# Keeping column-group products together on TensorE, with modulations two k-tiles at a time

## Chip, core and metric

The kernel runs on one core of a Trainium2 chip. The metric is the time of one execution in device microseconds; the time of a kernel is the median of its runs, and beside it stands one profiled execution, whose trace is read here.

## What is computed

A diffusion trunk of four layers over 256 latent and 256 context tokens of width 1024. Layer by layer the token mixer is windowed attention, a bidirectional Mamba-2, a bidirectional mLSTM and latent attention (MLA); after each comes a mixture of 16 small experts, two per token. Around every sub-layer the tokens are scaled, shifted and gated by a modulation, a linear map of the conditioning vectors:

```python
for i in range(DEPTH):
    mod_x = jax.nn.silu(c) @ w_mod[i] + b_mod[i]        # c: (1, 1024), w_mod[i]: (1024, 6144)
    mod_c = jax.nn.silu(c_ctx) @ w_mod[i] + b_mod[i]
    sh1x, sc1x, g1x, sh2x, sc2x, g2x = jnp.split(mod_x[:, None, :], 6, axis=-1)
    ...
    hx = rmsnorm(xs, norm1_g[i]) * (1.0 + sc1x) + sh1x
    yc, yx = mixer_i(hc, hx)                           # attention, Mamba-2, mLSTM, MLA
    xs = xs + g1x * yx
    hx = rmsnorm(xs, norm2_g[i]) * (1.0 + sc2x) + sh2x
    xs = xs + g2x * hier_moe(hx, ...)                  # the context tokens likewise
return rmsnorm(xs, final_norm_g)
```

All data is f32. The modulation weights are 24 MB a layer, read once each for two rows of input.

## The kernel before

Tokens stand as four tiles of 128 (two of context, two of latent). Large products use a split into two f32r halves and three products (`mm3`, lines 207 to 209); transposes and the small products of the mixers are plain f32. A compile-time scheduler sets the order of every engine's queue: it goes by the order of the program, takes work that its own estimate of time says is ready, and so interleaves work of different helpers. On the chip each engine then works through its queue in that order. Two means in the program bear on the order: `issue_after` ties the instructions of a block behind a given one on its engine, and `high_priority` lets a block go ahead of other ready work.

**Column groups.** A product whose result has only 32 or 64 rows fills 32 or 64 of TensorE's 128 columns. Such products are written to several groups of columns, each with its own rows of one PSUM bank, and groups can run side by side. Five places matter here:

- Modulations (line 231, tile `wm`): `mod_round(i, r)` computes a third (2048 columns) of layer i's modulation in eight steps, one per k-tile of 128 rows. A step loads one 1 MB tile `w` through `wload` (line 182, on SP's queue) and issues four products in four groups of 32 columns, each for 512 columns of the weights. After the eighth, `fin` adds the bias and spreads the result. There are three rounds a layer, 96 k-tiles in all.
- Attention values (line 1128): per token tile and key head, 4 or 8 products in two groups of 64 columns, for 2 or 4 key tiles `PT`.
- Mamba heads (line 1398): per pair of heads, 8 products, four chunks in two groups.
- mLSTM states (line 1635): 4 products in two groups, twelve times.
- MLA values (line 1927): per pair of heads, 8 products in two groups.

**Where modulations stand.** Round 0 of layer 0 runs at the start. The others are a list of steps, `fq`: rounds 1 and 2 of the layer and round 0 of the next. The mixers call `fill(n)` at fixed places, which takes n entries off the list; `drain` takes the rest at a mixer's end. The tiles `w` are a ring of four 1 MB buffers that modulation loads share with the weights of the mixers (and later of the experts), all issued on SP in one queue; a load waits for its buffer's last reader, and what is queued behind it waits too. In Mamba, SP's queue also carries the decay rows (`A`, line 1350; `E`, line 1354).

Of the kernel before, what the change touches and what calls it, by code (L numbers as in the profile page):

```python
# [23 lines left out]
class Trunk:  # L24
    def __init__(self, ctx, tc, I, K, out, slots=128, opts=None):
        self.ctx, self.tc, self.nc, self.I, self.K, self.out = ctx, tc, tc.nc, I, K, out
        self.o = dict(ring=4, eb=4, ob=6, wl=(8, 8, 8, 10), early=(5, 5, 3, 5), ahead=4, yb=3, fv=1, y0=0, mv=1, go=((0, 0), (1, 0), (2, 0), (0, 1), (3, 0), (1, 1), (2, 1), (3, 1)), cadd=(0, 512, 512, 0), mh=(8, 8, 4, 4), ms=3, mo=3, fm=(2, 2, 1, 0, 0, 0, 0, 6), sdp=0, pmw=1, pud=1, ac=1, fs=(3, 2, 2, 2, 1, 1, 1, 1, 2, 2, 2, 2, 1, 1, 2, 2), Mb=1, Wb=1, wa=4, fl=0, fc="1" * 16, fp=(4, 1), pg=(3,), pe=(0, 1, 2, 3), ptb=4, pb=8, n1p=0, lag=2, tl=4, cc=(1,), manual=False, stop=None)
        self.o.update(opts or {})
        self.C = slots
        self.fq, self.pending = deque(), None  # L30

# [165 lines left out]
    def split(self, pool, w, shape, name="split", bufs=3):  # L197
# [5 lines left out]
        return hi, lo  # L203

    def mm3(self, ps, a, b, start, stop):
        mm = self.nc.tensor.matmul
        mm(ps, a[0], b[0], start=start, stop=False)  # L207
        mm(ps, a[0], b[1], start=False, stop=False)  # L208
        self.last_mm = mm(ps, a[1], b[0], start=False, stop=stop)  # L209


    def mod_round(self, i, r):

        nc, I = self.nc, self.I
        st = {}

        def step(j, load=None):
            if j == 0:
                st["ps"] = self.P.tile([128, 512], F32, name="wm", bufs=1)
            if j == 6:  # L220
                st["b"] = (self.const if r == 2 else self.lay).tile([128, 512], F32, name=f"mod{r}", bufs=1)
                (nc.vector if self.o["mv"] else nc.gpsimd).memset(st["b"], 0.0)
                for s in range(2):
                    b = I["b_mod"]
                    src = bass.AP(tensor=b.tensor, offset=b.offset + i * 6 * D + r * 2048,
                                  ap=[[512, 4], [1, 512]])
                    nc.scalar.dma_start(st["b"][s:128:32, :], src)
            src = I["w_mod"][i].rearrange("(p j) n -> p j n", j=8)[:, j, r * 2048:(r + 1) * 2048]
            w = load([src]) if load else self.wload(src, [128, 2048])
            for g in range(4):  # L230
                nc.tensor.matmul(st["ps"][32 * g:32 * g + 32, :], self.cs[:, j, :], w[:, 512 * g:512 * g + 512],  # L231
                                 start=(j == 0), stop=(j == 7))

# [35 lines left out]

        return [lambda load=None, j=j: step(j, load) for j in range(8)] + [fin]  # L270

# [9 lines left out]
    def fill(self, n=1):  # L281
        for _ in range(n):
            if self.fq:
                self.fq.popleft()()

    def drain(self):
        while self.fq:
            self.fq.popleft()()

# [772 lines left out]
    def attn_core(self, pool, pout, kz, vr, qT):  # L1062
        nc, I, o = self.nc, self.I, self.o
# [44 lines left out]
        def values(t, kv, pr, sm):  # L1108

            nk = 2 if t < 2 else 4  # L1110
            tok = slice(t * 128, (t + 1) * 128)
            PT = [pool.tile([128, 2, 4, 128], F32, name="PT", bufs=o["ptb"]) for _ in range(nk // 2)]
            for g in range(4):
                p = pr[g][:, :nk * 128]
# [10 lines left out]
            po = self.core()  # L1125
            for k in range(nk):
                for par in range(2):
                    nc.tensor.matmul(po[par * 64:(par + 1) * 64, :256], vr[:, k, kv * 64:(kv + 1) * 64],
                                     PT[k // 2][:, k % 2, par::2, :], start=(k == 0), stop=(k == nk - 1))
            pv = po[:, :256].rearrange("p (m q) -> p m q", m=2)  # L1130
# [164 lines left out]
    def ssm_main(self, pool, late, mid, keep, heads):  # L1295
# [46 lines left out]
        def head(ft, zt, xs, xr, CT, Br, CB, gs, first):  # L1342
# [52 lines left out]
            py = self.core()  # L1395
            for c in range(4):
                for h in range(2):
                    nc.tensor.matmul(py[64 * h:64 * h + 64, tok(c)], xr[:, 128 * c + 64 * h:128 * c + 64 * h + 64],
                                     M[0][:, h, c, :], start=True, stop=True)
            y = xs  # L1400
# [208 lines left out]
    def mlstm_states(self, pool, keep, kT, va, gt):  # L1609
# [3 lines left out]
        st = {}  # L1613
# [12 lines left out]
        for d, order in ((0, (0, 1, 2, 3)), (1, (1, 0, 3, 2))):  # L1626
            for n in range(3):
                c, nx = order[n], order[n + 1]
                s = keep.tile([128, 4, 130], F32, name=f"cst{d}{n}")
                for ab in range(2):  # L1630
                    ps = self.core()
                    for a in (2 * ab, 2 * ab + 1):
                        for h in range(2):
                            hd = 2 * a + h
                            nc.tensor.matmul(ps[64 * h:64 * h + 64, (a % 2) * 130:(a % 2) * 130 + 130],
                                             kw[c, d][:, hd * 64:hd * 64 + 64], va[c][:, hd, :], start=True, stop=True)
                    for a in (2 * ab, 2 * ab + 1):
# [256 lines left out]
    def mla_core(self, pool, kT, vr, qT, ohi, olo):  # L1894
        nc, I = self.nc, self.I
        sc = 96.0 ** -0.5
        for a in range(8):
            po = self.core()
            PT = []
            for h in range(2):  # L1900
# [22 lines left out]
                PT.append(pt)  # L1923
            for k in range(4):
                for h in range(2):
                    hd = 2 * a + h
                    nc.tensor.matmul(po[64 * h:64 * h + 64, :256], vr[k][:, hd * 64:hd * 64 + 64],  # L1927
                                     PT[h][:, k].rearrange("p t q -> p (t q)"), start=(k == 0), stop=(k == 3))
            hh, ll = ohi[a // 2][:, a % 2, :], olo[a // 2][:, a % 2, :]
# [33 lines left out]
    def layers(self, dense=False):  # L1963
# [3 lines left out]
        for i in range(first, 4):  # L1967
# [3 lines left out]
            with self.pool("layer") as self.lay:  # L1971
                if i == first:
                    for n, f in enumerate(self.mod_round(i, 0)):
                        f()
                        if n == 3 and not dense:
                            self.load_x()
# [107 lines left out]
```

## Time and profile before

| what | value |
|---|---|
| median of 3 runs | 2065.24 us (2065.15 to 2068.01) |
| profiled execution | 2062.44 us |
| its span, first to last instruction | 2060.3 us |
| TensorE busy | 1899.6 us (92%) |
| VectorE, ScalarE, GpSimd busy | 1394.9, 1036.1, 536.4 us |
| mean granted TensorE clock | 0.963 of full speed |
| DMA, mean over the span | 229 GB/s |

In time order: start-up to 38 us, attention to 300, its experts to 500, Mamba to 950, its experts to 1170, mLSTM to 1460, its experts to 1700, MLA to 1880, and the last experts. Times in the trace count from the span's start. In a timeline of TensorE, PE is the products and PEld the weight loads that feed them; an f32 product appears as two records, an f32r product as one. A record's end is modelled and overlaps the next one's start, so costs are best read from start to start.

### The profile page before, as it was taken

How to read it: one execution, taken by the hardware profiler on the slowest of the kernel's cores; microseconds unless marked ns; L12 is line 12 of the kernel's file. 1: busy time of each engine (PE TensorE's matmuls, PEld its weight loads, DVE VectorE, ACT ScalarE, POOL GpSimd, SP SyncE). 2: the span in 40 equal slices, each digit the busy share in tenths (PEclk: the TensorE clock that was granted, in tenths of full speed). 3: DMA queues.
4: the chain of work that ended last, by engine and by line, in shares of the span. 5: the costliest groups of instructions: out<-in, count | busy, mean ns of one | idle time of the engine just before them, and what ended most of it. 6: DMA issues, size and time to landing. Idle time of an engine off the chain costs nothing. (4 is left out here: it accounts for less than half of the span.)

```text
span 2060.3 us, 30756 instructions
## 1 busy us (share of the span) xinstructions
PE 1899.6 (92%) x11036; PEld 1411.8 (69%) x11036; DVE 1394.9 (68%) x2728; ACT 1036.1 (50%) x2172; POOL 536.4 (26%) x525
## 2 busy tenths in 40 slices
PE   5999988999999999998799899996979999998996
PEld 2875686777767778776577678885867766656542
DVE  3568557886598787777788662338578876486444
ACT  2447526775575555433577542245457755454111
POOL 2012232213475555445221410004241132001000
PEclk8999998999999999999899999998989999999998
DMA  9344667986486546547798557542669966807792
GB/s 342 137 164 166 244 208 275 400 304 191 135 252 210 158 169 200 180 141 269 266 391 339 164 163 265 189 164 90 236 215 378 401 194 228 296 11 277 285 368 94
DMA packets 172915, 471.73 MB, mean 229 GB/s; under 512 B 27769, under 2 KB 74993, under 8 KB 152272
## 3 DMA queue, kind: packets, MB, share of 16 engines
q1 hardware_dynamic: 148912, 401.98, 54.3%
q0 software_dynamic: 23136, 65.86, 10.0%
q8 instruction: 90, 1.47, 0.3%
q10 hardware_dynamic: 704, 1.82, 0.2%
q14 instruction: 73, 0.60, 0.1%
HBM read 452.41 MB, written 29.77 MB: 234 GB/s over the span
## 5 line engine op out<-in xcount | busy, mean ns | idle before, releaser
L758 DVE TENSOR_TENSOR elo<-wl,ehi 128x1024 fp32r<-128x1024 f32 x156 | 187.0, 1220 | 27.8 <-ACT ehi L757 26.9
L757 ACT ACTIVATE ehi<-wl 128x1024 fp32r<-128x1024 f32 x156 | 161.6, 1055 | 51.8 <-PE acc L209 32.7
L231 PE MATMUL wm<-w,cs 128*32 128x512 f32 x768 | 125.2, 640 | 22.7 <-DMA w<-in_w_mod_dram 22.7
L763 POOL DMA_INDIRECT xg<-hd,gi x48 | 64.0, 1334 | 281.9 <-PE tr L776 224.0
L1292 POOL TENSOR_TENSOR wcl<-w,wch 128x512 fp32r<-128x512 f32 x76 | 114.2, 1515 | 81.8 <-ACT wch L1291 75.7
L207 PE MATMUL acc<-hhi,wch 128*128 128x512 f32 (+1 forms) x336 | 131.8, 393 | 0.5 <-ACT wch L1291 0.5
L209 PE MATMUL acc<-split_hi,hlo 128*128 128x256 f32 x464 | 131.3, 285 | 0.0
L209 PE MATMUL acc<-hhi,wcl 128*128 128x512 f32 (+1 forms) x336 | 129.8, 388 | 1.4 <-POOL wcl L1292 1.4
L208 PE MATMUL acc<-split_lo,hhi 128*128 128x256 f32 x464 | 131.0, 285 | 0.0
L207 PE MATMUL acc<-split_hi,hhi 128*128 128x256 f32 x464 | 131.0, 286 | 0.0
L208 PE MATMUL acc<-hlo,wch 128*128 128x512 f32 (+1 forms) x336 | 129.9, 387 | 0.0
L207 PE MATMUL acc<-ehi,xTh 128*128 128x512 f32 x288 | 123.6, 429 | 2.2 <-ACT xTh L779 2.2
L208 PE MATMUL acc<-elo,xTh 128*128 128x512 f32 x288 | 117.8, 409 | 1.1 <-DVE elo L758 1.1
L209 PE MATMUL acc<-ehi,xTl 128*128 128x512 f32 x288 | 115.6, 401 | 0.0
L758 DVE TENSOR_TENSOR elo<-w,ehi 128x1024 fp32r<-128x1024 f32 x84 | 100.9, 1218 | 13.6 <-ACT ehi L757 13.1
L757 ACT ACTIVATE ehi<-w 128x1024 fp32r<-128x1024 f32 x84 | 87.0, 1052 | 26.2 <-PE acc L209 14.8
L1370 ACT ACTIVATE A<-A,lnb 128x128 f32<-128x128 f32 x256 | 78.6, 388 | 39.4 <-POOL A L1365 39.4
L207 PEld LDWEIGHTS acc<-split_hi,hhi 128*128 128x128 f32 x464 | 88.1, 191 | 9.4 <-issue 3.5
L202 DVE TENSOR_TENSOR split_lo<-w,split_hi 128x1024 fp32r<-128x1024 f32 x33 | 40.1, 1224 | 80.3 <-ACT split_hi L201 80.0
L209 PEld LDWEIGHTS acc<-split_hi,hlo 128*128 128x128 f32 x464 | 88.5, 191 | 3.2 <-DVE split_lo L202 0.8
L386 POOL TENSOR_TENSOR x<-x,restmp 128x256 f32<-128x256 f32 (+1 forms) x46 | 48.2, 1047 | 160.1 <-DVE restmp L382 146.0
L208 PEld LDWEIGHTS acc<-split_lo,hhi 128*128 128x128 f32 x464 | 88.5, 191 | 0.7 <-issue 0.7
(625 smaller groups left out, 5456.9 us busy)
## 6 DMA issues: line engine op xcount, KB each, us to landing
w<-in_w_mod_dram SPq DMA_DIRECT2D x96, 1024.0 KB
wl<-in_moe_w_down_dram SPq DMA_DIRECT2D x47, 1024.0 KB
wl<-in_moe_w_gate_dram SPq DMA_DIRECT2D x82, 512.0 KB
wl<-in_moe_w_up_dram SPq DMA_DIRECT2D x82, 512.0 KB
w<-in_moe_w_gate_dram SPq DMA_DIRECT2D x46, 512.0 KB
w<-in_moe_w_up_dram SPq DMA_DIRECT2D x46, 512.0 KB
w<-in_ssm_w_in_dram SPq DMA_DIRECT2D x40, 512.0 KB
yd<-y POOLq DMA_DIRECT2D x39, 512.0 KB, 9.6
```

The costliest lines, as they stand in the source:

```text
L202: self.nc.vector.tensor_sub(lo, w, hi)
L207: mm(ps, a[0], b[0], start=start, stop=False)
L208: mm(ps, a[0], b[1], start=False, stop=False)
L209: self.last_mm = mm(ps, a[1], b[0], start=False, stop=stop)
L231: nc.tensor.matmul(st["ps"][32 * g:32 * g + 32, :], self.cs[:, j, :], w[:, 512 * g:512 * g + 512], start=(j == 0), stop=(j == 7))
L386: (nc.vector if last else nc.gpsimd).tensor_add(x, x, tmp)
L757: nc.scalar.activation(hi, v, AF.Copy)
L758: nc.vector.tensor_sub(lo, v, hi)
L763: nc.gpsimd.indirect_dma_start(out=xgs[e % len(xgs)], out_offset=None, in_=self.hd, in_offset=bass.IndirectOffsetOnAxis(ap=self.gi[:, e:e ...
L1292: (eng or self.nc.gpsimd).tensor_sub(lo, v, hi)
L1370: nc.scalar.activation(M[d][:, h, c], M[d][:, h, c], AF.Exp, bias=self.lb[:, c, k:k + 1])
```

## The change

A new helper, `together`, issues the first of a list of products as usual and ties the others behind it with high priority. It is used at the five places above. In the attention values the products run over the key tiles from last to first, and in the MLA values the second head of a pair comes first. A modulation step now covers two k-tiles: it issues two loads and then eight products through `together`; the list `fq` holds four such steps and `fin` a round, each with the number of old steps it stands for, and `fill` adds to a credit and takes an entry when the credit covers it. At the start, `load_x` is called after the second double step instead of the fourth single one. Arithmetic and data are the same.

```diff
+    def together(self, jobs):
+        jobs = list(jobs)
+        first = jobs[0]()
+        with self.tc.issue_after(first.ins), self.tc.high_priority():
+            for m in jobs[1:]:
+                m()
...
-            src = I["w_mod"][i].rearrange("(p j) n -> p j n", j=8)[:, j, r * 2048:(r + 1) * 2048]
-            w = load([src]) if load else self.wload(src, [128, 2048])
-            for g in range(4):
-                nc.tensor.matmul(st["ps"][32 * g:32 * g + 32, :], self.cs[:, j, :], w[:, 512 * g:512 * g + 512],
-                                 start=(j == 0), stop=(j == 7))
+            ws = []
+            for jj in (j, j + 1):
+                src = I["w_mod"][i].rearrange("(p j) n -> p j n", j=8)[:, jj, r * 2048:(r + 1) * 2048]
+                ws.append(load([src]) if load else self.wload(src, [128, 2048]))
+            self.together(lambda g=g, k=k: nc.tensor.matmul(
+                st["ps"][32 * g:32 * g + 32, :], self.cs[:, j + k, :], ws[k][:, 512 * g:512 * g + 512],
+                start=(j + k == 0), stop=(j + k == 7)) for k in range(2) for g in range(4))
...
-        return [lambda load=None, j=j: step(j, load) for j in range(8)] + [fin]
+        return [(2, lambda load=None, j=j: step(j, load)) for j in range(0, 8, 2)] + [(1, fin)]
...
     def fill(self, n=1):
-        for _ in range(n):
-            if self.fq:
-                self.fq.popleft()()
+        self.credit += n
+        while self.fq and self.credit >= self.fq[0][0]:
+            k, f = self.fq.popleft()
+            f()
+            self.credit -= k
...
-            for k in range(nk):
-                for par in range(2):
-                    nc.tensor.matmul(po[par * 64:(par + 1) * 64, :256], vr[:, k, kv * 64:(kv + 1) * 64],
-                                     PT[k // 2][:, k % 2, par::2, :], start=(k == 0), stop=(k == nk - 1))
+            self.together(lambda k=k, par=par: nc.tensor.matmul(
+                po[par * 64:(par + 1) * 64, :256], vr[:, k, kv * 64:(kv + 1) * 64],
+                PT[k // 2][:, k % 2, par::2, :], start=(k == nk - 1), stop=(k == 0))
+                for k in range(nk - 1, -1, -1) for par in (1, 0))
...
-            for c in range(4):
-                for h in range(2):
-                    nc.tensor.matmul(py[64 * h:64 * h + 64, tok(c)], xr[:, 128 * c + 64 * h:128 * c + 64 * h + 64],
-                                     M[0][:, h, c, :], start=True, stop=True)
+            self.together(lambda c=c, h=h: nc.tensor.matmul(
+                py[64 * h:64 * h + 64, tok(c)], xr[:, 128 * c + 64 * h:128 * c + 64 * h + 64],
+                M[0][:, h, c, :], start=True, stop=True) for c in range(4) for h in range(2))
...
-            for k in range(4):
-                for h in range(2):
-                    hd = 2 * a + h
-                    nc.tensor.matmul(po[64 * h:64 * h + 64, :256], vr[k][:, hd * 64:hd * 64 + 64],
-                                     PT[h][:, k].rearrange("p t q -> p (t q)"), start=(k == 0), stop=(k == 3))
+            self.together(lambda k=k, h=h: nc.tensor.matmul(
+                po[64 * h:64 * h + 64, :256], vr[k][:, (2 * a + h) * 64:(2 * a + h) * 64 + 64],
+                PT[h][:, k].rearrange("p t q -> p (t q)"), start=(k == 0), stop=(k == 3))
+                for k in range(4) for h in (1, 0))
```

Line numbers move with the change: modulation products stand on line 241 instead of 231, attention values on 1141 (1128), Mamba's on 1411 (1398), mLSTM states on 1646 (1635), MLA values on 1937 (1927); other lines move by 8 to 15. Counted over the whole queue of TensorE, modulations stand in 91 unbroken runs before and 60 after (32 of one k-tile, 24 of two, 2 of four, the rest at the start), attention values in 31 and 16, Mamba's in 30 and 16, mLSTM states in 11 and 11, MLA values in 15 and 8. Three places show how.

TensorE's queue in a Mamba head before: `wm` are modulation products, `tr<-CT,st` and `core<-ud,Br` products of the head's states, `acc<-hhi,wch` and the like the split products of the next projection; x5 is five products in a row.

```order
L208 MATMUL acc<-hlo_5255,wch 128x512
L209 MATMUL acc<-hhi_5253,wcl 128x512
L231 MATMUL wm<-w,cs 32x512 x5
L1393 MATMUL tr<-CT,st_6154 128x128
L231 MATMUL wm<-w,cs 32x512 x3
L1379 MATMUL core<-ud,Br 128x128 x2
```

The same two k-tiles after:

```order
L216 MATMUL acc<-hlo_5255,wch 128x512
L217 MATMUL acc<-hhi_5253,wcl 128x512
L241 MATMUL wm<-w,cs 32x512 x8
L215 MATMUL acc<-hhi_5252,wch 128x512
L216 MATMUL acc<-hlo_5254,wch 128x512
L217 MATMUL acc<-hhi_5252,wcl 128x512
```

Eight products that stood in two runs, of five and three, stand in one.

TensorE's queue in the attention core before, for one token tile and key head: `core<-PT,vr` are the values, `tr<-ident,p` transposes of the probabilities, `acc<-kh,qT` and `acc<-kl,qT` the scores of the next head, `mj` the mask.

```order
L1128 MATMUL core<-PT,vr 64x256
L1118 MATMUL tr<-ident,p 128x128 x4
L1088 MATMUL acc<-kh_210,qT_217 128x512
L1088 MATMUL acc<-kl_211,qT_217 128x512
L1093 LDWEIGHTS identb
L1093 MATMUL acc<-mj_1354,identb 128x128
L1128 MATMUL core<-PT,vr 64x256 x7
```

After:

```order
L1103 MATMUL acc<-kh_210,qT_217 128x512
L1103 MATMUL acc<-kl_211,qT_217 128x512
L1108 LDWEIGHTS identb
L1108 MATMUL acc<-mj_1354,identb 128x128
L1141 MATMUL core<-PT,vr 64x256 x8
L1133 MATMUL tr<-ident,p 128x128 x4
```

The first of the eight no longer stands apart, ahead of a group of transposes and scores.

TensorE's queue at the end of the mLSTM before: `acc<-va,SD` and `core<-cst,qz` are the last token tile's products, `tr<-ident,mod` belongs to `fin`.

```order
L1700 MATMUL acc<-va_11699,SD 128x130 x2
L231 MATMUL wm<-w,cs 32x512 x11
L1704 MATMUL core<-cst_13046,qz_13603 128x130
L1704 MATMUL core<-cst_13076,qz_13603 128x130
L231 MATMUL wm<-w,cs 32x512 x9
L240 MATMUL tr<-ident,mod_14286 128x128 x4
```

After:

```order
L1713 MATMUL acc<-va_11699,SD 128x130 x4
L241 MATMUL wm<-w,cs 32x512 x16
L1717 MATMUL core<-cst_13036,qz_13597 128x130
L1717 MATMUL core<-cst_13066,qz_13597 128x130
L241 MATMUL wm<-w,cs 32x512 x8
L251 MATMUL tr<-ident,mod_14286 128x128 x4
```

Twenty modulation products, five k-tiles, were left for this place; now it is twenty-four, six k-tiles.

## Rows read from the trace of the kernel before

**Rows 1.** The page: busy time, share and instructions of each engine; DMA.

```profile
PE 1899.6 (92%) x11036; PEld 1411.8 (69%) x11036; DVE 1394.9 (68%) x2728; ACT 1036.1 (50%) x2172; POOL 536.4 (26%) x525
...
DMA packets 172915, 471.73 MB, mean 229 GB/s; under 512 B 27769, under 2 KB 74993, under 8 KB 152272
```

**Rows 2.** Table of stretches: length, busy time by engine, granted clock, DMA share, GB/s.

```profile
145.00:250.00 105.00, 102.44 (x674) 57.87 (x672) 74.11 (x226) 73.29 (x242) 25.61 (x21) 1.00 0.56 196
...
750.00:850.00 100.00, 100.00 (x533) 75.80 (x533) 77.15 (x116) 52.78 (x126) 56.84 (x42) 1.00 0.58 190
...
1435.00:1460.00 25.00, 19.36 (x138) 13.84 (x136) 18.07 (x54) 14.57 (x51) 7.37 (x10) 0.93 0.90 336
...
1800.00:1870.00 70.00, 68.23 (x355) 38.13 (x354) 55.99 (x158) 39.88 (x98) 0.86 (x2) 1.00 0.21 71
```

**Rows 3.** Timeline of TensorE, attention core: start, length, engine, line, product, records.

```profile
199.63 1.08 PE L1128 MATMUL core<-PT,vr 128*64 128x256 f32 x8
...
204.94 1.07 PE L231 MATMUL wm<-w,cs 128*32 128x512 f32 x8
205.94 0.66 PE L1118 MATMUL tr<-ident,p 128*128 128x128 f32 x4
206.52 0.65 PE L1128 MATMUL core<-PT,vr 128*64 128x256 f32 x2
...
208.82 1.94 PE L1128 MATMUL core<-PT,vr 128*64 128x256 f32 x14
```

**Rows 4.** The same timeline in the attention projections.

```profile
51.30 1.04 PE L231 MATMUL wm<-w,cs 128*32 128x512 f32 x2
```

**Rows 5.** The same timeline in the mLSTM's projections.

```profile
1293.71 0.28 PE L208 MATMUL acc<-split_lo,hhi 128*128 128x256 f32 x1
1293.83 0.28 PE L209 MATMUL acc<-split_hi,hlo 128*128 128x256 f32 x1
1294.04 1.92 PE L231 MATMUL wm<-w,cs 128*32 128x512 f32 x16
1295.90 0.39 PE L207 MATMUL acc<-split_hi,hhi 128*128 128x256 f32 x1
```

**Rows 6.** The same timeline in a Mamba head.

```profile
784.77 1.09 PE L1398 MATMUL core<-A,xr 128*64 128x128 f32 x16
```

**Rows 7.** Stretches, lines 231 (four rows), 1128, 1398, 1927 alone: TensorE busy, weight loads.

```profile
38.00:300.00 262.00, 27.90 (x192) 4.38 (x192) 0.98 0.54 190
500.00:950.00 450.00, 35.96 (x192) 5.65 (x192) 0.99 0.58 187
1170.00:1460.00 290.00, 27.24 (x192) 4.86 (x192) 0.96 0.53 186
1700.00:1880.00 180.00, 19.75 (x128) 3.10 (x128) 0.97 0.53 191
...
38.00:300.00 262.00, 33.72 (x192) 15.02 (x192) 0.98 0.54 190
...
500.00:950.00 450.00, 22.91 (x256) 15.52 (x256) 0.99 0.58 187
...
1700.00:1880.00 180.00, 20.69 (x128) 9.90 (x128) 0.97 0.53 191
```

**Rows 8.** SP's issues, TensorE's wait at the mLSTM's end, and its waits in sum.

```profile
61.83 4.91 SPq L182 DMA_DIRECT2D w<-in_w_mod_dram  x2
...
1437.09 0.33 SPq L182 DMA_DIRECT2D w<-in_w_mod_dram  x1
...
1442.03 1.07 PE L231 MATMUL wm<-w,cs 128*32 128x512 f32 x8 [0.81 <-DMA w<-in_w_mod_dram]
...
PE wm L231 <- DMA w<-in_w_mod_dram: 22.7, 11, 6.8
```

**Rows 9.** Timeline of weight loads in the run of Rows 5; idle before in brackets.

```profile
1294.50 0.13 PEld L231 LDWEIGHTS wm<-w,cs 128*32 128x32 f32 x4 [0.30 <-issue]
1294.93 0.13 PEld L231 LDWEIGHTS wm<-w,cs 128*32 128x32 f32 x4 [0.30 <-issue]
```

More of the change, by code (lines that the diff above doesn't have):

```diff
@@ L29, in __init__ @@
         self.C = slots
-        self.fq, self.pending = deque(), None
+        self.fq, self.pending, self.credit = deque(), None, 0
     def setup(self):
@@ L281, in fill @@
     def fill(self, n=1):
-        for _ in range(n):
-            if self.fq:
-                self.fq.popleft()()
+        self.credit += n
[3 more added lines that the diff above has]
+            self.credit -= k
     def drain(self):
         while self.fq:
-            self.fq.popleft()()
+            self.fq.popleft()[1]()
+        self.credit = 0
     def rstd(self, x, junk, n=D):
@@ L1631, in mlstm_states @@
                     ps = self.core()
-                    for a in (2 * ab, 2 * ab + 1):
-                        for h in range(2):
-                            hd = 2 * a + h
-                            nc.tensor.matmul(ps[64 * h:64 * h + 64, (a % 2) * 130:(a % 2) * 130 + 130],
-                                             kw[c, d][:, hd * 64:hd * 64 + 64], va[c][:, hd, :], start=True, stop=True)
+                    self.together(lambda a=a, h=h: nc.tensor.matmul(
+                        ps[64 * h:64 * h + 64, (a % 2) * 130:(a % 2) * 130 + 130],
+                        kw[c, d][:, (2 * a + h) * 64:(2 * a + h) * 64 + 64], va[c][:, 2 * a + h, :],
+                        start=True, stop=True) for a in (2 * ab, 2 * ab + 1) for h in range(2))
                     for a in (2 * ab, 2 * ab + 1):
@@ L1923, in mla_core @@
                 PT.append(pt)
-            for k in range(4):
-                for h in range(2):
-                    hd = 2 * a + h
-                    nc.tensor.matmul(po[64 * h:64 * h + 64, :256], vr[k][:, hd * 64:hd * 64 + 64],
-                                     PT[h][:, k].rearrange("p t q -> p (t q)"), start=(k == 0), stop=(k == 3))
+            self.together(lambda k=k, h=h: nc.tensor.matmul(
+                po[64 * h:64 * h + 64, :256], vr[k][:, (2 * a + h) * 64:(2 * a + h) * 64 + 64],
+                PT[h][:, k].rearrange("p t q -> p (t q)"), start=(k == 0), stop=(k == 3))
+                for k in range(4) for h in (1, 0))
             hh, ll = ohi[a // 2][:, a % 2, :], olo[a // 2][:, a % 2, :]
@@ L1972, in layers @@
                 if i == first:
-                    for n, f in enumerate(self.mod_round(i, 0)):
+                    for n, (_, f) in enumerate(self.mod_round(i, 0)):
                         f()
-                        if n == 3 and not dense:
+                        if n == 1 and not dense:
                             self.load_x()
```

## The prediction

> **What bounds the kernel now.** I read the page first. TensorE is busy for 1899.6 us, 92% of the span, VectorE for 68% [rows 1]. The table of stretches then shows whether anything else comes close where the change acts: in the attention core (145 to 250 us) TensorE is busy 102.44 of 105 us against 74.11 of VectorE, in the Mamba heads 100 of 100 against 77.15, in the MLA core 68.23 of 70 against 55.99 [rows 2]. So in these stages TensorE's own queue sets the time, and an interval taken out of it shortens the run until VectorE or a dependent chain takes over. One stretch is different: at the end of the mLSTM (1435 to 1460) TensorE is busy 19.36 of 25 us while the DMA engines are 90% busy at 336 GB/s [rows 2].
>
> Then I read the timeline of TensorE for what a product in column groups costs. Each f32 product stands there as two records, its two passes. The eight records of one modulation k-tile (four groups) start at 204.94 and the next product starts at 205.94: 1.00 us [rows 3]. Eight records are busy 1.07 us [rows 3], two records, one group alone, 1.04 [rows 4]. **A lone group costs as much as all four**, because the four run side by side. Two k-tiles unbroken, 16 records, take from 1294.04 to 1295.90, 1.86 us instead of 2.00; and the step into the column groups costs too: ordinary products of 256 columns follow each other after 0.12 us (1293.71 to 1293.83), the first modulation product comes 0.21 us after the last of them [rows 5]. So each visit costs about 0.09 going in and 0.14 on leaving and refilling, and each broken-off piece costs a whole k-tile. The 64-column products behave alike: two records alone are busy 0.65 us, while the other 14 of that product group take a busy 1.94 and eight unbroken ones 1.08 [rows 3]; in the Mamba heads all 16 unbroken take 1.09 [rows 6].
>
> **The change, part by part.** I count runs of column-group products in the order of before and after, and price them with the busy time of a run. That time holds about 0.07 us at its end that lies under the next product (1.07 busy against 1.00 to the next start), and leaves out the 0.09 of the way in; the two nearly cancel, so I use busy time as it stands.
>
> 1. *Modulations.* Before, 96 k-tiles stand in 91 runs, two of them in the start-up; the 89 others are busy 27.90 (attention), 35.96 (Mamba), 27.24 (mLSTM) and 19.75 us (MLA) [rows 7]. After, there are 60 runs, 58 past the start-up: 32 single k-tiles, 24 pairs and 2 double pairs. Not every pair stays together, since the order puts other products between the halves of 16 pairs. At 1.07, 1.92 and, by adding two more steps of 0.86 (1.86 less 1.00), 3.64 us a run, the attention layer comes to 8x1.07 + 6x1.92 + 3.64 = 23.7, Mamba to 6x1.07 + 9x1.92 = 23.7, mLSTM to 4x1.07 + 8x1.92 + 3.64 = 23.3, MLA to 14x1.07 + 1.92 = 16.9. Saved: 4.2, 12.3, 3.9 and 2.9, together 23.3 us. Most of it is the pieces of one to three groups that go, not the switches alone.
>
> 2. *Attention values* (line 1128). Before 31 runs busy 33.72 us [rows 7], after 16: eight of eight records at 1.08 and eight of sixteen. Sixteen does not occur undisturbed in the trace; I take the 1.94 of fourteen, since a pair of groups costs the same with one member missing. 8x1.08 + 8x1.94 = 24.2; saved 9.5. The turned order of the products starts with the probabilities that come last, so the run holds no wait inside it; the lone product that ran ahead of them did nothing that shortened the rest (14 records take 1.94, as four full pairs do).
>
> 3. *Mamba* (line 1398): 30 runs busy 22.91 us [rows 7], after 16 at 1.09 [rows 6] = 17.4; saved 5.5. *MLA values* (line 1927): 15 runs busy 20.69 us [rows 7], after 8 at 1.94 = 15.5; saved 5.2. *mLSTM states*: 11 runs before and 11 after; I take nothing.
>
> Sum out of TensorE's queue: 13.7 us in attention, 17.8 in Mamba, 3.9 in mLSTM, 8.1 in MLA, **43.5 us**. What of it becomes time: in attention and MLA I take nine tenths (12.3 and 7.3), because VectorE runs at 70 to 80% there and softmax chains end some waits; in Mamba 0.93 (16.5); in the mLSTM nine tenths (3.5). VectorE, at 77.15 of 100 in the Mamba heads, would stand at some 81 after the cut, so it does not become the bound.
>
> Costs. *The double loads.* A step now issues two 1 MB loads on SP and takes two of the four ring tiles at once. Queued behind a load that waits for its tile are the next weights, and in Mamba also the decay rows. In the order of after SP's rows are almost unchanged, so I bound this from two rows. In the attention projections two k-tiles are now used where the queue stands at about 68 and 72 us instead of 89 and 103, and before their loads went out between 61.83 and 66.74 [rows 8]. Their tiles also come free earlier now. Bounds: nothing, or about one load time each, 1 MB at the 229 GB/s of the page = 4.6 us [rows 1], so 0 to 9 us. I take 1, nearer to zero, because all waits of TensorE on such a load come to 22.7 us in eleven times, 6.8 of them in one wait at the start; the one at 1442 is 0.81 [rows 8]. *mLSTM's end.* Before, five k-tiles are left there and the ring holds four, so one load goes out at 1437.09, after the first tile is free, and is used at 1442.03. After, six are left (the order shows 24 products instead of 20), so two loads go out late, and the output weights wait behind them. At 336 GB/s one more MB is 3.1 us [rows 2]; bounds 0 (other waits there cover it) and 3.1; I take 3. The credit counter itself only shifts a step to the next call; the start-up, where both orders are the same, costs what it did.
>
> Net: 12.3 - 1 + 16.5 + 3.5 - 3 + 7.3 = 35.6 us. The profiled execution took 2062.4 us, 2060.3 of them span; the median of the runs is 2065.2, 2.8 above it. 2062.4 - 35.6 is 2026.8, or against the median **2029 us**.
>
> **A rule weighed against a row.** In the run of two k-tiles the weight loads of the second begin at 1294.50 and 1294.93, while passes of the same columns run on all 128 rows [rows 5 and 9]; they are hidden. The Trainium skill (TensorE: Matmul & The Clock Gate, Part 3, "The mechanism") says that a weight load overlaps products in flight only when the row group differs. By it each of the 30 places where two k-tiles now join (88 k-tiles in 58 runs) would pay its two loads of 0.13 us, 7.8 us in all, and the time would be 2037. The trace does not agree.
>
> **The rivals.**
>
> *Given back to the softmax chains and the other engines.* If in the attention and MLA cores, and in the heads, only half of the cut becomes time, 43.5/2 less the 4 of loads leaves 18 us: 2047. For it: every PSUM bank is freed by ScalarE or VectorE, and VectorE is at 70 to 80%. Against it: TensorE is 97 to 100% busy in just these stretches [rows 2].
>
> *Second tile late* (slower). All products of a pair are queued behind its first one, so a second k-tile whose load has not landed holds TensorE with everything behind it. One such wait costs up to a load, 4.6 us. The gain of 39.6 us without the 4 of loads already taken is used up by nine late pairs of 48; with thirteen it is about 20 us slower, 2085. For it: two of four ring tiles per step, and the mLSTM's end, where exactly this happens. Against it: SP's order hardly moves, the order itself parts 16 pairs whose second tile it expects late, and in the attention core and the heads the DMA engines are busy 56 and 58% [rows 2]. Five to nine late pairs would end within 0.2%.
>
> *Loads at the joins not hidden*: 2037, as above, with little behind it.
>
> *The change does not do what it says*: a part of this is certain (16 pairs parted, mLSTM's states unchanged) and is in the sum.
>
> **How the numbers follow.** Forecast 0.68, between 2014 (all 43.5 us, and some 7 us of waits inside the broken runs gone too) and 2042; half given back 0.16, 2047; unhidden loads 0.03, 2037; late tiles up to the gain 0.06, about 2065; more of them 0.07, 2085. About 0.2% (4 us) is what a measurement of this kernel can tell from no change. Faster by more than that: 0.68 + 0.16 + 0.03 = 0.87; within it 0.06; slower 0.07. The range 2013 to 2050 leaves out the last two cases and the tails.
>
> **What would show it.** Busy time of TensorE down by about 40 us, with unchanged work; modulations at some 87.6 us past the start-up instead of 110.85; line 1128's products near 24, 1398's near 17.4, MLA's near 15.5. Mamba (first modulation to router) shorter by 15 to 18 us, attention by 10 to 13, MLA by 6 to 8, the mLSTM nearly as long as before. Wrong would be: waits on modulation loads beyond the start-up and the mLSTM's end (late tiles); or busy time down as said but idle time of TensorE up by as much, ended by ScalarE or VectorE (given back); or a run of two k-tiles over 2.0 us.

## The result and the profile after

The changed kernel takes 2026.86 us (median of four runs, 2025.83 to 2030.94) against 2065.19 us before: a ratio of 0.982, 95% interval 0.9805 to 0.9834, **38 us faster**; the forecast was 2029 us. The profiled execution has a span of 2024.0 us, 36.3 less than before. The page's line of busy times and its row of modulation products, then the two of TensorE's waits that matter here (us in total, times, longest):

```profile
PE 1858.6 (92%) x11036; PEld 1400.7 (69%) x11036; DVE 1394.1 (69%) x2728; ACT 1034.1 (51%) x2172; POOL 538.7 (27%) x525
...
L241 PE MATMUL wm<-w,cs 128*32 128x512 f32 x768 | 104.3, 645 | 22.1 <-DMA w<-in_w_mod_dram 22.1
```

```profile
PE wm L241 <- DMA w<-in_w_mod_dram: 22.1, 10, 6.6
...
PE acc L1103 <- ACT p L1113: 4.9, 7, 1.8
```

Against [rows 1], TensorE is busy 41.0 us less, with the same 11036 records; VectorE and ScalarE are as busy as they were. The waits on modulation loads are what they were [rows 8]. The table of stretches for the lines of [rows 7], now 241 (four rows), 1141, 1411 and 1937, each with its length, TensorE's busy time on that line alone, its weight loads, the granted clock, the DMA share and GB/s:

```profile
38.00:300.00 262.00, 23.93 (x192) 4.72 (x192) 0.97 0.55 197
480.00:945.00 465.00, 23.70 (x192) 4.69 (x192) 1.00 0.61 196
1140.00:1450.00 310.00, 24.37 (x192) 4.84 (x192) 0.96 0.55 188
1665.00:1860.00 195.00, 16.84 (x128) 2.62 (x128) 0.97 0.56 197
...
38.00:300.00 262.00, 24.25 (x192) 12.36 (x192) 0.97 0.55 197
...
480.00:945.00 465.00, 17.51 (x256) 13.64 (x256) 1.00 0.61 196
...
1665.00:1860.00 195.00, 15.58 (x128) 8.48 (x128) 0.97 0.56 197
```

The forecast said 23.7, 23.7, 23.3 and 16.9 for the modulations, and 24.2, 17.4 and 15.5 for the others. Every term is met within 0.3 us but the mLSTM's modulations, 1.1 us over. Two rows of TensorE's timeline, one in the mLSTM's projections and one in the attention core, show runs that did not occur or were rare before, each with the product that follows it:

```profile
1266.23 1.92 PE L241 MATMUL wm<-w,cs 128*32 128x512 f32 x16
1268.08 0.39 PE L215 MATMUL acc<-split_hi,hhi 128*128 128x256 f32 x1
...
211.67 1.95 PE L1141 MATMUL core<-PT,vr 128*64 128x256 f32 x16
213.55 0.66 PE L1133 MATMUL tr<-ident,p 128*128 128x128 f32 x4
```

Two k-tiles take 1.85 us to the next start, against 1.86 in [rows 5], and sixteen value records 1.88 us: the price of fourteen in [rows 3] was the right one.

So the sum is right, 43.5 us said and 41.0 found in TensorE's busy time. How it turned into time is the question. I cut each trace at the same events (first product of a router, first transpose of a norm, first product `acc<-va,SD` in the mLSTM's core); "experts" is from a router to the next norm, and the attention column starts with the program. All in us:

```
              attention experts  Mamba  experts  mLSTM    mLSTM   experts   MLA   experts   span
                                               projections core
before          294.5    203.1   473.6   205.8   197.6    128.3    203.7   187.4   166.4   2060.3
after           287.6    203.3   454.4   207.7   192.8    124.7    205.9   180.2   167.4   2024.0
difference       -6.9     +0.2   -19.2    +1.9    -4.8     -3.6     +2.2    -7.2    +1.0    -36.3
forecast        -11.3      0     -16.5     0        -0.5 together     0     -7.3     0      -35.6
```

Mamba and MLA are near, attention is 4.4 us short, the mLSTM gained 8 us that nobody had promised, and the experts lost 5.

### The profile page after: what moved, and what is told of

The parts are those of the page before. It is cut to its first block, busy times and chain, and to the rows that moved or that the text cites. A ratio compares the mean times of both kernels' runs of the same rounds, so it can differ in the third digit from the quotient of the medians.

```text
span 2024.0 us, 30759 instructions
## 1 busy us (share of the span) xinstructions
PE 1858.6 (92%) x11036; PEld 1400.7 (69%) x11036; DVE 1394.1 (69%) x2728; ACT 1034.1 (51%) x2172; POOL 538.7 (27%) x525
## 3 DMA queue, kind: packets, MB, share of 16 engines
q0 software_dynamic: 23136, 65.86, 10.2%
## 5 line engine op out<-in xcount | busy, mean ns | idle before, releaser
L241 PE MATMUL wm<-w,cs 128*32 128x512 f32 x768 | 104.3, 645 | 22.1 <-DMA w<-in_w_mod_dram 22.1
```

Source lines behind the costliest of these rows:

```text
L241: self.together(lambda g=g, k=k: nc.tensor.matmul(st["ps"][32 * g:32 * g + 32, :], self.cs[:, j + k, :], ws[k][:, 512 * g:512 * g + 512], ...
```

## The experiments

**The change's halves.** First each kind of product alone. For the modulations alone, the mixers' products stand as in the kernel before; for the products alone, a modulation step is one loose k-tile as before. The lines below show both against the changed kernel.

```diff
@@ e_mods, the four places of the mixers (attention shown)
-            self.together(lambda k=k, par=par: nc.tensor.matmul(
...
+            for k in range(nk):
+                for par in range(2):
+                    nc.tensor.matmul(po[par * 64:(par + 1) * 64, :256], vr[:, k, kv * 64:(kv + 1) * 64],
@@ e_prods, step(j)
-            for jj in (j, j + 1):
...
-            self.together(lambda g=g, k=k: nc.tensor.matmul(
...
+            for g in range(4):
+                nc.tensor.matmul(st["ps"][32 * g:32 * g + 32, :], self.cs[:, j, :], w[:, 512 * g:512 * g + 512],
```

> The change with its modulations alone: steps of two k-tiles kept together; the products of attention, Mamba, mLSTM and MLA stand as before. Theory (time comes from TensorE's queue, in every place for itself): the modulations' busy time falls from 110.85 to about 87.6 us past the start-up as in the changed kernel, Mamba's stage ends 12 to 13 us sooner, attention's 2 to 4, MLA's 2 to 3; the kernel is 17 to 21 us faster than before, 2044 to 2048. Rival (the modulations only fill idle time of TensorE, the gain is in the mixers' products): under 5 us faster, 2060 or more.

> The change with the mixers' products alone: attention values, Mamba's, mLSTM's states and MLA's values kept together, modulations in single loose steps as before. Theory: busy time of these products as in the changed kernel (24.25, 17.51 and 15.58 us), Mamba's stage 5 to 6 us shorter, MLA's 4 to 5, attention's 4 to 8; 14 to 19 us faster than before, 2046 to 2051, and together with the modulations alone about the whole 38 us. Rival (both parts are needed, since a run is broken by the other kind): the two parts alone give less than half of the whole, 2058 or more here.

Modulations alone: 2049.25 us, ratio 0.9937 (0.9918 to 0.9956), just above the expected 2044 to 2048. Products alone: 2046.56, 0.9917 (0.9887 to 0.9946), as expected. Beside them the kernel before took 2063.6, so the parts add up to 14 + 17 = 31 of some 37 us. But their stages do not add up: Mamba's 473.6 us are 470.0 with the modulations alone, 469.1 with the products alone and 454.4 with both. The 12 to 13 us that the modulations alone were to bring there did not come: TensorE is busy 449.35 us of the stage instead of 458.59, but idles 5.7 us more. With single k-tiles (next) the parts nearly add up: Mamba is 13.0 us shorter with the modulations alone, 4.5 with the products alone and 15.2 with everything.

**Single k-tiles.** Half of the change's words are about two k-tiles at a time. This kernel takes one k-tile a step, one load, its four products kept together; the second one does the same with all the change's other products.

```diff
@@ e_mods_one and e_one_all, step(j)
-            for jj in (j, j + 1):
...
-            self.together(lambda g=g, k=k: nc.tensor.matmul(
...
+            self.together(lambda g=g: nc.tensor.matmul(
+                st["ps"][32 * g:32 * g + 32, :], self.cs[:, j, :], w[:, 512 * g:512 * g + 512],
+                start=(j == 0), stop=(j == 7)) for g in range(4))
```

> The modulations in single k-tiles as before, one load a step, but the four products of a k-tile kept together; the mixers' products as before. By the order of its queue the modulations stand in 74 runs with no pieces of one to three groups; at 1.07 us a k-tile and 0.86 for each further one they would be busy some 3 us more than with pairs. Theory (it is the pieces that cost, a switch only 0.23 us): 14 to 18 us faster than before, 2047 to 2051, within 5 us of the modulations in pairs. Rival (the saving is in half as many switches): less than half of what the pairs give, 2056 or more.

> The changed kernel with all its unbroken products, but a modulation step loads and multiplies one k-tile, whose four products are kept together, as in the run of modulations alone with single k-tiles. Counted in the order, the modulations stand in 74 runs instead of 60. Theory (each switch costs, as the prediction priced it at 0.14 us a run and more with the way in): TensorE busy 2 to 3 us more, time 2029 to 2031. Rival (pairs bring nothing in all: pieces were the cost, and a step of twice the length holds up what is queued behind it; modulations alone were 6.8 us faster with single k-tiles): 2019 to 2024.

Modulations alone with single k-tiles: 2042.48 us, 0.9901 (0.9871 to 0.9931), below the expected 2047 to 2051 and 7 us below the pairs; a difference of that size can come from the order alone, as the mLSTM shows below. Everything with single k-tiles: 2028.08, 0.9831 (0.9801 to 0.9861), between the two expected ranges and the same as the changed kernel. Modulations are busy 106.1 and 107.0 us there against 105.0 and 104.3 with pairs. So pairs, which stand in 60 runs instead of 74, save 1 to 3 us of TensorE, and no time that these runs show. **Whole k-tiles are the modulations' gain; two at a time are not.** The attention core shows one reason. Table of stretches from the first scores to the output weights: length, busy time of TensorE, its weight loads, VectorE, ScalarE and GpSimd, granted clock, DMA; before, single k-tiles, pairs (the changed kernel), and four at a time (below):

```profile
129.90:245.90 116.00, 108.79 (x691) 61.14 (x687) 83.71 (x268) 78.76 (x262) 30.92 (x29) 0.96 0.52 183
```

```profile
127.70:236.60 108.90, 99.62 (x690) 58.12 (x686) 83.60 (x267) 77.57 (x262) 31.04 (x29) 0.95 0.52 179
```

```profile
127.60:238.90 111.30, 99.28 (x688) 59.21 (x686) 84.09 (x269) 76.92 (x262) 30.67 (x30) 0.95 0.48 176
```

```profile
127.70:245.80 118.10, 102.78 (x688) 60.84 (x686) 83.38 (x270) 77.97 (x262) 31.10 (x30) 0.94 0.45 169
```

Length less busy time is what TensorE idles: 7.2, 9.3, 12.0 and 15.3 us. From the first row to the second only the values differ, the modulations are busy 17.57 us in both. From the second on only the modulation step grows, and with it TensorE's wait for the exponentials: 2.5 us with single k-tiles, 4.9 with pairs (above), 6.3 with four.

```profile
PE acc L1101 <- ACT p L1111: 2.5, 3, 1.1
```

```profile
PE acc L1103 <- ACT p L1113: 6.3, 8, 1.8
```

So the longer a modulation step, the longer TensorE waits for the softmax around it. Pairs shorten the modulations in the core by 2.2 us (15.40) and lengthen the core by 2.4. This repeats: with the modulations in loose single steps and the values together, the core takes 108.6 and 109.0 us (values alone, products alone), and in a second kernel with pairs (one pair moved, below) 111.2.

**Four at a time.** The steps and the credit of the queue go from two to four.

```diff
@@ e_quad
-            for jj in (j, j + 1):
+            for jj in (j, j + 1, j + 2, j + 3):
...
-        return [(2, lambda load=None, j=j: step(j, load)) for j in range(0, 8, 2)] + [(1, fin)]
+        return [(4, lambda load=None, j=j: step(j, load)) for j in range(0, 8, 4)] + [(1, fin)]
```

> The changed kernel, but a modulation step issues four loads and multiplies four k-tiles, so that it asks for all four tiles of the ring at once. Counted in the order, the modulations stand in 62 runs instead of 60, so the busy time should be the same within 1 us. Theory (the loads' place in the queues does not matter as long as the order parts a step whose tiles are late): 2025 to 2031. Rival (late tiles, as in the prediction: every product of a step is queued behind its first one, and the third and fourth tile come a load of 4.6 us each later): waits of TensorE on modulation loads by tens of us, 2040 to 2070.

2064.0 us, ratio 1.0 (0.9985 to 1.0014): the whole gain is gone, with the modulations busy as little as in the changed kernel. Its row on the page, then two of TensorE's waits:

```profile
L241 PE MATMUL wm<-w,cs 128*32 128x512 f32 x768 | 104.2, 640 | 26.5 <-DMA w<-in_w_mod_dram 26.4
```

```profile
PE tr L1758 <- DVE A L258: 6.2, 1, 6.2
PE acc L1713 <- DVE num L1724: 6.2, 3, 3.1
```

The rival's time came, but not by its mechanism alone. Waits on late tiles grew by 4.3 us only, not by tens of us: 1.0 in attention, 2.2 at the mLSTM's end and 1.1 in MLA. More came behind them: in the mLSTM from its first `acc<-va,SD` to the router it is 142.0 us instead of 124.7, where the output's transposes wait 6.2 us, as they do not in the changed kernel, for VectorE's A, which is made from the late modulations. The attention stage is 6.9 us longer; in its core TensorE idles 3.3 us more and is 3.5 us longer busy with the same products. Mamba is 10.5 us longer from norm to router, and the mean clock is 0.954 instead of 0.965. How much of this is the clock, the run does not tell.

**Two loads without unbroken products.** The kernel before, with two loads and two loose k-tiles in a step.

```diff
@@ e_loads, step(j)
+            for jj in (j, j + 1):
...
+                w = load([src]) if load else self.wload(src, [128, 2048])
+                for g in range(4):
```

> The kernel before with one part of the change alone: a modulation step issues two loads and two k-tiles, but no products are kept together, so that pieces stay: 81 runs of modulation products instead of 91, of 121 us by the prediction's prices instead of 118. Theory (the loads two at a time cost next to nothing, pieces are what costs): like before or up to 4 us slower, 2062 to 2068. Rival (a step taken two k-tiles at a time is worth something by itself, since there are half as many switches): 6 to 12 us faster, 2052 to 2058.

2069.84 us, 1.0024 (1.001 to 1.0038): 5 us slower than before, and 2 above the expected range. The modulations are busy 128.6 us, 3.4 more than before; if all of that became time, some 2 us are left for the loads by themselves, of which the forecast took 1. Its waits on modulation loads are 21.1 us against 22.7 [rows 8].

**The attention's values.** Only they are kept together, the rest is as before:

```diff
@@ e_attn, values(t, kv, pr, sm)
-            for k in range(nk):
-                for par in range(2):
-                    nc.tensor.matmul(po[par * 64:(par + 1) * 64, :256], vr[:, k, kv * 64:(kv + 1) * 64],
...
+            self.together(lambda k=k, par=par: nc.tensor.matmul(
...
+                for k in range(nk - 1, -1, -1) for par in (1, 0))
```

> The attention values alone kept together, in their turned order; everything else as before. TensorE has 9.5 us less to do in the attention core. The prediction's step (nine tenths of it becomes time): 8.6 us faster than before, 2056 to 2057. What the changed kernel's trace suggests (about half is given back as waits of TensorE on ScalarE's probabilities and their copies): 4 to 5 us faster, 2060 to 2061, with the idle time of TensorE between 130 and 245 us up by 4 to 5.

2047.48 us, 0.9928 (0.9903 to 0.9953): a miss, 16 us where 8 or 4 were expected. The attention stage explains half: 287.1 us, 7.4 less, close to the forecast's nine tenths of 9.5. The rest lies in stages whose code is untouched, most of it in the mLSTM: its core takes 119.8 us instead of 128.3, of which the experts behind it lose 4.0 again; Mamba and MLA are 2.8 and 3.0 us shorter. I come to that below.

**The order of the values.** The changed kernel takes the last k-tile first. This one keeps them together in natural order.

```diff
@@ e_natural, values(t, kv, pr, sm)
-                PT[k // 2][:, k % 2, par::2, :], start=(k == nk - 1), stop=(k == 0))
-                for k in range(nk - 1, -1, -1) for par in (1, 0))
+                PT[k // 2][:, k % 2, par::2, :], start=(k == 0), stop=(k == nk - 1))
+                for k in range(nk) for par in (0, 1))
```

> The changed kernel, but the attention's value products stand together in their natural order (first k-tile first). They then follow an earlier p-tile by one product, so that 13 of the 16 blocks begin with a lone product that runs ahead: 29 runs in the attention instead of 16. Theory (a lone product costs 0.65 us busy and shortens the rest by nothing, and the queue of TensorE sets the time): 13 x 0.65 = 8.4 us more busy, 4 to 8 us slower, 2031 to 2035. Rival (TensorE waits for the last probabilities there anyway, 12 us idle in the core, so the lone products are hidden): 2026 to 2028.

2041.62 us, 0.9894 (0.9862 to 0.9927): 15 us slower than the changed kernel, where 4 to 8 were expected. The values are busy again as before, and TensorE idles less for it; line 1141 alone in the core, then the core with all engines:

```profile
128.00:244.30 116.30, 33.54 (x192) 15.44 (x192) 0.96 0.44 162
```

```profile
128.00:244.30 116.30, 107.92 (x689) 61.97 (x687) 83.32 (x270) 77.65 (x262) 30.25 (x30) 0.96 0.44 162
```

The lone product that runs ahead costs its full run: 33.54 us against 24.25. The attention stage is 5.3 us longer, which is the cost that the theory named. The other 11 of the 16.2 us between the two profiled spans are not in the attention: Mamba +4.3, mLSTM +4.9, its experts +1.9, the same code as in the changed kernel.

**Where attention's gain went.** In the changed kernel's core TensorE waits for ScalarE's exponentials and copies. Two kernels ask whose queue it is. The first moves a quarter of the copies to VectorE, the second leaves out VectorE's scaling of the probabilities.

```diff
@@ e_pe, options
-pe=(0, 1, 2, 3)
+pe=(0, 1, 2)
@@ e_noscale, values(t, kv, pr, sm)
-                (nc.gpsimd if g in o["pg"] else nc.vector).tensor_scalar(p, p, sm[:, g:g + 1], None, op0=OP.mult)
+                if g in o["pg"]:
+                    nc.gpsimd.tensor_scalar(p, p, sm[:, g:g + 1], None, op0=OP.mult)
```

> The changed kernel, but in the attention core one in four copies of transposed probabilities (PT) is made by VectorE instead of ScalarE: 24 copies, some 9 us, move over. In the changed kernel's core TensorE waits 4.9 us in seven times for ScalarE's exponentials and 1.9 us in six for its copies. Theory (ScalarE's queue is what gave back half of the values' 9.5 us): those waits go, the core is 2 to 5 us shorter, 2022 to 2025. Rival (the chain goes through VectorE's row maxima as well, which has 84 of 111 us filled and would get 93): the waits only change their name, 2026 to 2032.

> The changed kernel with work left out: in the attention core the scaling of the probabilities by VectorE is not done (three heads of four, 48 operations, 22.9 us of VectorE), so the values are not normalised there. Everything else stands. Read is the core, 111.3 us from the first scores to the weights of the output, with TensorE idle for 12 us of it. Theory (VectorE's share of the softmax chain gave back half of what the values' products saved): TensorE's waits for exponentials and copies go, the core takes 105 to 108 us. Rival (it is the length of the chain from score to maximum to exponential, which the scaling is no part of, and the three score tiles): the wait for exponentials stays near 4.9 us and the core at 110 to 112 us.

Less ScalarE: 2042.41 us, 0.99 (0.9883 to 0.9916), slower than both expected ranges, and the core is longer. Less VectorE: 2024.7 us, 0.9801 (0.9782 to 0.9819), and the core is shorter, as the theory said. The stretch and the waits of TensorE in it, first of the one, then of the other:

```profile
127.60:241.70 114.10, 101.32 (x690) 59.67 (x689) 91.32 (x294) 71.68 (x238) 31.36 (x30) 0.96 0.47 173
```

```profile
PE acc L1103 <- ACT p L1113: 5.0, 6, 1.8
PE core L1141 <- DVE PT L1139: 2.1, 4, 0.8
```

```profile
127.60:234.40 106.80, 99.20 (x691) 59.85 (x689) 64.64 (x221) 76.39 (x262) 27.46 (x30) 0.94 0.46 165
```

```profile
PE acc L1103 <- ACT p L1113: 2.6, 3, 1.8
...
PE core L1142 <- ACT PT L1138: 0.8, 3, 0.3
```

With ScalarE at 71.68 us instead of 76.92 the wait that names ScalarE stays at 5.0 us, and the one for its copies only changes its name; VectorE carries 7.2 us more in this run (91.32 against 84.09). With VectorE at 64.64 the wait halves, and the 116.00 us of before become 106.80, 9.2 us less, nearly all that TensorE is relieved of there (108.79 to 99.20). **The wait names ScalarE, but VectorE stands behind it.** The groups of ScalarE's exponentials tell how: busy time, mean, and the idle time ahead of them with what ended it, in the changed kernel and without the scaling:

```profile
L1113 ACT ACTIVATE p<-acc,nm 128x512 f32<-128x512 f32 x32 | 22.3, 702 | 5.2 <-DVE nm L1111 3.4 <-DVE sm L1119 1.1 <-PE wm L241 0.7
L1113 ACT ACTIVATE p<-acc,nm 128x256 f32<-128x256 f32 x32 | 15.1, 475 | 6.9 <-DVE nm L1111 6.8
```

```profile
L1113 ACT ACTIVATE p<-acc,nm 128x512 f32<-128x512 f32 x32 | 22.0, 703 | 5.0 <-PE wm L241 2.5 <-DVE nm L1111 2.5
L1113 ACT ACTIVATE p<-acc,nm 128x256 f32<-128x256 f32 x32 | 15.1, 474 | 3.5 <-DVE nm L1111 2.7 <-DVE sm L1118 0.5 <-DVE sm L1119 0.2
```

The exponentials idle 10.2 us for VectorE's row maxima (nm) in the one and 5.2 in the other: the maxima stand behind the scaling in VectorE's queue. That the scaling is also a step of the chain to the transposes, this run does not part from it. What it won in the attention it lost again in the mLSTM (+6.4 us), so the total hardly moved.

**The mLSTM.** Two kernels: the state products alone kept together in the kernel before (eleven runs either way), and one pair of modulations moved from the mLSTM's end into its blocks, so that the ring holds what is left.

```diff
@@ e_st, the states
-                    for a in (2 * ab, 2 * ab + 1):
...
+                    self.together(lambda a=a, h=h: nc.tensor.matmul(
@@ e_fm, options
-fm=(2, 2, 1, 0, 0, 0, 0, 6)
+fm=(2, 2, 2, 0, 0, 0, 0, 5)
```

> The kernel before with one part of the change alone: the mLSTM's state products kept together. Their runs stay 11, only 25 rows of TensorE's queue stand otherwise, none of any other engine. Theory (this part is worth nothing, and what shortened the mLSTM's core by 5 us in the changed kernel is VectorE's order, which this kernel keeps): same as before, 2063 to 2066, mLSTM core as long as before. Rival (the states' order made the mLSTM's core shorter): 3 to 5 us faster, 2059 to 2062.

> The changed kernel, but one more pair of modulation k-tiles is given to the mLSTM's blocks and one fewer to its end, so that four k-tiles, as many as the ring of weight tiles holds, are left at the end instead of six. The work is the same. Theory (the two late loads hold TensorE 3.4 us at the mLSTM's end, and no other wait covers all of it): 2023.5 to 2025.5. Rival (the products behind them waited for VectorE anyway and now wait again): 2026 to 2028.

States alone: 2063.06 us, 1.0001 (0.9986 to 1.0015), worth nothing, as the forecast took it. The profiled run had a span of 2054.7 us all the same, 5.6 under before's; more on that below. One pair earlier: 2032.31 us, 0.984 (0.9807 to 0.9873), outside both expected ranges and not faster. Before the mLSTM it has the changed kernel's order on every engine, and its profiled run is 2.9 us behind there; the mLSTM and its experts added 4.0. The rows of the changed kernel's mLSTM end, then the waits there with the pair moved:

```profile
1402.37 3.64 PE L241 MATMUL wm<-w,cs 128*32 128x512 f32 x32
...
1408.63 1.07 PE L241 MATMUL wm<-w,cs 128*32 128x512 f32 x8 [1.97 <-DMA w<-in_w_mod_dram]
...
1411.15 1.94 PE L241 MATMUL wm<-w,cs 128*32 128x512 f32 x8 [1.45 <-DMA w<-in_w_mod_dram]
```

```profile
PE tr L1758 <- DVE ml L1763: 2.5, 1, 2.5
PE core L1717 <- ACT inter L1723: 2.2, 1, 2.2
PE acc L215 <- ACT woh L420: 1.1, 1, 1.1
```

The two late loads (1.97 + 1.45 us) are gone. A wait of 2.2 us for ScalarE now stands ahead of the last modulations and one of 2.5 for VectorE's `ml` behind them, where the changed kernel waits 0.3. So other waits cover the loads here; that the chain through the gates and norms sets the end of the mLSTM is my reading of these waits and not tested.

## Why the prediction was right, and where it was not

**The sum.** Right in each term but the mLSTM's modulations (1.1 us over), since runs were counted in the order and priced by runs of the same length in the trace of before. The price of a join held too: four k-tiles unbroken are busy 3.64 us in the mLSTM's end above, three steps of 0.86 over 1.07. The rival of loads at the joins that are not hidden falls with that; the Trainium skill's rule (TensorE: Matmul & The Clock Gate, Part 3, "The mechanism"), as the prediction applies it, does not hold in these runs of column groups.

**Attention.** The mechanism was right and the size was off: nine tenths of 13.7 were taken, and 6.9 us came. The step that failed is the one that turned busy time into time there. TensorE's 102.44 of 105 us [rows 2] say that its queue set the pace before; they do not say how much can be cut before the softmax sets it, and about half was the limit. The two parts of the cut fared differently. The values together shorten the core by 7.4 us where nothing else is changed (116.0 to 108.6), nearly eight tenths of 9.5; the row of that kernel:

```profile
129.80:238.40 108.60, 99.30 (x690) 57.66 (x686) 83.45 (x267) 77.58 (x262) 30.97 (x29) 0.97 0.53 179
```

The 4.2 us of the modulations brought no time: the first scores come 2.3 us sooner, and the pairs take 2.4 back in the core. That a longer unbroken step itself holds up the softmax has no term in the sum. The rival "given back to the softmax chains" was right for this core, and the run without the scaling shows by whom: VectorE.

**Mamba.** 16.5 us forecast. Before's own profile is a little slow here, 473.6 us, where two other kernels with the same Mamba code show 470.6 and 470.8. Five with the changed Mamba show 454.4 to 458.7, 455.9 in the mean. Against the mean of the three, 471.7, that is 15.8 us.

**mLSTM.** The forecast was -0.5 us, the two traces differ by -8.4, and the run with the values of attention alone gained as much in an mLSTM that it does not touch. Four kernels share the changed kernel's mLSTM code, three that of before (one of them with the states together); core and the experts behind it, us:

```
before 128.3 + 203.7   values alone 119.8 + 207.7   states alone 125.1 + 202.5
after  124.7 + 205.9   natural order 129.6 + 207.8   copies moved 129.3 + 208.8   scaling left out 131.1 + 202.4
```

With the projections added the first three come to 529.6, 525.0 and 524.7, the others to 523.4, 530.2, 530.9 and 526.3. The means, 526.4 and 527.7, differ by 1.3 us, where the forecast said -0.5; the spread inside the rows is 4.9 and 7.5 us. What differs inside a row is the order of the instructions, which the scheduler sets anew when something far ahead moves, and the clock. Two kernels of the second row, natural order and copies moved, have the mLSTM in the same order on every engine, and their cores are 0.3 us apart. **So the -8.4 are mostly a draw**: a lucky order after, an unlucky one before. In the means the projections gain 4.6 us (197.4 to 192.8) and the core loses 4.3, close to the 3.5 and 3 of the forecast. But that the core's loss is the two late loads is not shown: without them (one pair moved) it took 125.7 us.

**Taken together** the agreement within 2 us is better than the working deserves: attention was 4.4 too high, and the draw in the mLSTM made up for it and for the experts' 5. These 5 are no larger than what unchanged code shows elsewhere: Mamba's experts take 205.8 us with the values in natural order and 211.8 with the scaling left out. The variants of the changed kernel, corrected by their difference in the attention stage alone, lie at 2027 (the changed kernel), 2029, 2032, 2036 and 2040 us. An estimate from these five is a gain of about 30 us, with 6 or 7 to either side from order and clock; the changed kernel itself is the best of them.

**The other rivals.** Late tiles did not decide it: waits on modulation loads are 22.1 us against 22.7. At four k-tiles a step the gain is gone, and late loads are a part of that; where between two and four it turns, no run here shows.

## What to carry to other kernels

Count broken runs of column-group products and price them from the trace: here a lone group costs as much as all four, keeping one k-tile's products together brought the modulations' whole gain, and longer steps held up the softmax beside them. Where an engine is at 97%, ask how far the next one lets the cut go before taking nine tenths of it, and find out who stands behind a wait by taking work off each engine, since the name on the wait may be that of a middleman. And where a scheduler sets the order, read a stage in several variants with the same code before explaining 5 us of it.

## What the runs showed of the hardware beyond that

The granted clock goes with differences as large as a small edit's. Over 19 runs of the kernel before, one and the same program, the fastest took 2060.81 us at a mean clock of 0.968 and the slowest 2069.84 at 0.959. It can be seen in one stretch of Mamba's heads, first in the profile of before, then with the states alone kept together, where all queues stand in the same order; TensorE idles 1.3 us of it in the one and 1.6 in the other:

```profile
600.00:620.00 20.00, 18.72 (x94) 13.93 (x93) 19.96 (x31) 14.41 (x37) 12.99 (x10) 0.91 0.65 207
```

```profile
600.00:620.00 20.00, 18.36 (x99) 13.78 (x98) 19.96 (x32) 14.56 (x37) 14.08 (x11) 1.00 0.71 234
```

One ran part of it below the upper level of 2.4 GHz (0.91 in the mean), the other all of it at that level; from first head to router they took 406.2 and 403.7 us. What decides which way it goes, no run here shows.
